# Two transformer blocks on one core: grouped attention products, early splits of the attention output, and the context's first modulation moved behind the last split of block 1

## The chip, the cores and the metric

The kernel runs on 1 core of one Trainium2 chip. The metric is the device time of one execution in microseconds (us). The engines are called by the profile's names: PE does the matrix products, DVE the elementwise work, ACT the functions of one input, POOL some elementwise work and DMA issues, SP issues most DMAs.

## The reference, cut to what matters

Two blocks run one after the other over 512 tokens of width 1024. Block 1 is one layer whose halves are an RWKV-7 recurrence (8 heads) and a stick-breaking attention (8 heads):

```python
h = rmsnorm(x, norm_g[l]) * (1.0 + scale[:, None, :]) + shift[:, None, :]
p = h @ w_in[l]
y = jnp.concatenate([y_rwkv, y_sb], axis=-1) @ w_out[l]
x = x + gate[:, None, :] * y
return rmsnorm(x, final_g)
```

Block 2 has two layers. Beside x it carries a context of 256 tokens, which has a modulation of its own. Layer 0 mixes with a short convolution, layer 1 with neighbourhood attention (16 heads, a window of keys and all of the context), and each ends in a gated feed-forward:

```python
h = _modulate(_rms_norm(x, norm_mix[i]), sh1, sc1)
hc = _modulate(_rms_norm(ctx, norm_mix[i]), sh1c, sc1c)
...
s = jnp.concatenate([s_win.reshape(bsz, N_HEADS, GRID_W, kh * GRID_W), s_ctx], axis=-1)
p = jax.nn.softmax(s, axis=-1).astype(v.dtype)
...
x = x + g1 * y
x = x + g2 * _swiglu(_modulate(_rms_norm(x, norm_ffn[i]), sh2, sc2), ffn_w_in[i], ffn_w_out[i])
```

Everything is fp32.

## The kernel before, in words

Activations lie transposed: eight tiles of 128 channels by 512 tokens for x, eight of 128 by 256 for the context (xc). A large product is made of three: each operand is split into a high part in the shorter format fp32r (a copy on ACT) and the low rest (a subtraction on DVE), and `mm3` (L172 to L174) adds high by high, high by low and low by high in one PSUM bank. `split_w` (L155, L156) does this for weights as they arrive by DMA in the SP queue; four slots hold 512-column pieces of split weights, so two weight tiles of 1024 columns are at hand at a time. `split` (L307, L308) does it for activations, and `modulate` (L288 to L291) for a normed and modulated tile: a product `nt` on DVE, a cast with the shift on ACT, a difference on DVE.

The kernel is written against a scheduler that lays out each engine's queue when the program is built. It takes ready instructions by the order of the program, with its own model of durations, so work that comes later in the text fills gaps of earlier work. `order(later, earlier)` adds an edge between two instructions that only this planning sees; no semaphore comes of it. Tiles with one tag share a fixed number of slots, and a tile waits for its slot. PSUM has eight banks, shared out by tag: in block 1 `acc` has two and six other tags have one each; in layer 1 `acc` 2, `cacc` 1, `sm` 2, `pt` 2, `py` 1.

The end of block 1 (`block1`, from L398). The output product takes the eight parts y in the order `YORD`, so y3 and y7 come last. The loop over `YORD` splits each part (h0 to h7 by name); when it comes to y3 it first issues the products of the six parts at hand for all eight output tiles (`part`), and loads `w2`, the weights of the last two parts. Ahead of that loop stands the context's norm and its `modulate` (tiles nt, hc0 to hc7), which layer 0 needs first. Behind the loop, for each of the eight output tiles, the products with y3 and y7 (h3, h7) follow, an addition into x (L452), a square on ACT (L455) and a weighted sum of squares (L458, L460) that a product with a matrix of ones closes into the bank `ss` (L462). Its inverse root (`rsqrt`: Ln, then Exp, both on ACT) is r, with which layer 0's h is modulated.

The last stick-breaking pair (`sb_pair(3)`) runs beside the last RWKV pair. Its Sigmoids (L1154, L1155) and the Ln and Exp of the RWKV pair's norm (L242, L249) need different function tables of ACT.

In `layer0` the sum of all squares (`self.scale`, L491) is added up on DVE beside the first products. These start with the context (`lead`, `ctx_first`).

Layer 1 (`layer1`) runs eight pairs of heads (`na_pair`). Each pair makes q and k, norms them, and then goes through four blocks of 128 queries: for each of its two heads the scores (L863, L864, bank `sm`), the bias and the row minimum on DVE (L868), Exp on ACT (L870), the scaling by the inverse sum on POOL (L872), four transposes on PE (L876, bank `pt`) and a copy out (L877). After every second block `na_values` multiplies with the values (L896, bank `py`). Output parts 0 to 6 are copied to `o0` to `o6` and split after the last pair, into slots of the attention's own tags; part 7 is split straight from PSUM. Then `attn_w_out` is multiplied, one output tile m after the other, with the last two in halves of 256 tokens, each followed by the addition into x (L769) and a square. The modulation for the feed-forward (`turn`) follows by halves.

The feed-forward (`ffn`, with `split=1` in layer 1) begins with `lead`, which makes gate and up product of hidden tile 0 in both `acc` banks. For tile i, `gemm2` makes the gate product, then Tanh on ACT (L643), a product on DVE (L644), the up product, and a product and split (L649, L307, L308).

Of the kernel before, what the change touches and what calls it, by code (L numbers as in the profile page):

```python
# [16 lines left out]
KT = 8  # L17
# [67 lines left out]
class K:  # L85
# [198 lines left out]
    def modulate(self, xs, ks, gain, mod, sh0, r, h, pool, tag, rstd, bufs=2):  # L284
        nc, n = self.nc, rstd.shape[1]
        for k in ks:
# [4 lines left out]
            nc.vector.scalar_tensor_tensor(h[k][1], t, sh, h[k][0].bitcast(F32),  # L291
                                           op0=ALU.add, op1=ALU.subtract)
# [17 lines left out]
    def block1(self):  # L310
# [68 lines left out]
        with self.open(name="sb", bufs=1) as sb:  # L379
# [22 lines left out]
            with self.open(name="tail", bufs=2) as tp:  # L402
# [9 lines left out]
                self.modulate(xc, range(KT), gc, mod, 0, 1, hc, tp, "cz", rstd)  # L412
                yh, part = [], []
                for k in YORD:
# [31 lines left out]
        for n, m in enumerate((6, 7, 0, 1, 2, 3, 4, 5)):  # L446
# [10 lines left out]
            if n == 0:  # L457
                nc.vector.tensor_scalar(acc, sq, fw[:, m:m + 1], None, op0=ALU.mult)  # L458
            elif n <= 5:
                nc.vector.scalar_tensor_tensor(acc, sq, fw[:, m:m + 1], acc, op0=ALU.mult, op1=ALU.add)  # L460
            if n >= 5:
                nc.tensor.matmul(ms, lhsT=self.C("ones") if n == 5 else fwt[:, n - 6], rhs=acc if n == 5 else sq,  # L462
                                 start=n == 5, stop=n == 7)
# [8 lines left out]
        self.modulate(xs, range(KT), g, mod, 0, 0, h, pool, "xz", r2)  # L472

    def layer0(self):
# [13 lines left out]
        for i in range(8):  # L488
            zs.append(self.conv_tile(i, st, pool, lead if i == 0 else None))
            if i < 7:  # L490
                nc.vector.tensor_add(self.scale, self.sqs[0] if i == 0 else self.scale, self.sqs[i + 1])  # L491
# [65 lines left out]
    def gemm2(self, src, h, hc, k0=0, k1=KT):  # L557
        po = self.psum("acc")
# [71 lines left out]
    def ffn(self, l, st, pool, parts, fin=None, split=0):  # L630
# [51 lines left out]
    def xgemm(self, src, h, k0=0, k1=KT):  # L682
        out = self.psum("acc")
# [22 lines left out]
    def layer1(self):  # L706
# [5 lines left out]
        with ExitStack() as es:  # L712
# [34 lines left out]
            os = [pool.tile([128, S], F32, name=f"o{k}") for k in range(KT - 1)] + [None]  # L747
# [530 lines left out]
```

## Time and profile before

| what | value |
|---|---|
| median of 3 runs | 2077.85 us (2076.53 to 2081.96) |
| the profiled execution's own time | 2080.14 us |
| its span, first to last instruction | 2078.4 us |
| granted TensorE clock, mean | 0.994 |
| end of block 1 and turn to layer 0 | about 455 to 515 us of the span |
| attention of layer 1 | about 1425 to 1665 us |
| output product and turn to the last feed-forward | about 1665 to 1729 us |

The profile is of one execution. A row of its timeline gives the start in us from the span's start, the duration, the engine, the line, the operation, what it writes and reads, the shapes and the count, and in brackets how long the engine had been idle and whose end it waited for. A matrix product's duration includes its drain, which overlaps with the next one; the rate is read from start to start. PEclk is the share of the TensorE clock that was granted.

### The profile page before, as it was taken

To read this page: it belongs to the slowest core of one execution; us is meant where nothing else is said; L and a number is where in the kernel's file an instruction comes from. 1 tells how busy PE (TensorE), PEld (TensorE's weight loads), DVE (VectorE), ACT (ScalarE), POOL (GpSimd) and SP (SyncE) were. 2 spreads that over 40 slices of the span, in tenths; PEclk is the share of its full clock that TensorE was granted. 3 is DMA by queue.
4 is the path that set the end of the run, shared out by engine and by line. 5 is a ranking of instruction groups with operands and counts; after the bars stand their busy time and mean duration, and the time that the engine had idled before them with its cause. 6 is when DMAs were issued, how large, how long until landed. Compare 5 with 4: busy or idle time off the path is not lost.

```text
span 2078.4 us, 33492 instructions
## 1 busy us (share of the span) xinstructions
PE 2029.1 (98%) x13564; PEld 1637.2 (79%) x13564; DVE 1230.9 (59%) x2641; ACT 795.6 (38%) x1493; POOL 131.5 (6%) x212
## 2 busy tenths in 40 slices
PE   6999999998999999999999999999999999999999
PEld 3766667666888888888888888898777687888887
DVE  2869888658766738675446343444666754444443
ACT  3536444446322224221222222335776743323232
POOL 0000000000000000000001000001223200000000
PEclk9999999999999999999999999999999999999999
DMA  7432222122233312344235221122111122323323
GB/s 280 150 113 92 94 74 93 40 81 83 92 122 122 122 61 93 131 133 151 94 135 177 72 96 61 58 82 67 56 52 51 36 82 82 101 93 97 98 98 103
DMA packets 61355, 203.59 MB, mean 98 GB/s; under 512 B 6928, under 2 KB 8976, under 8 KB 61200
## 3 DMA queue, kind: packets, MB, share of 16 engines
q1 hardware_dynamic: 45360, 145.77, 21.6%
q0 software_dynamic: 15120, 55.06, 8.1%
q8 instruction: 106, 1.74, 0.4%
q10 hardware_dynamic: 720, 0.62, 0.1%
q14 instruction: 49, 0.40, 0.1%
HBM read 199.32 MB, written 2.10 MB: 97 GB/s over the span
## 4 chain that ended last, share of the span: by engine, by line
PE 87%; ACT 3%; DVE 3%; issue 1%; POOL 0%; DMA 0%; POOLq 0%; DVEq 0%; ACTq 0%
PE acc L173 20%; PE acc L174 20%; PE acc L172 19%; PE cacc L174 5%; PE cacc L173 5%; PE cacc L172 5%; PE py L896 2%; PE pT L876 1%; PE ss L1150 1%; PE so L1172 1%; PE sm L863 1%; PE sm L864 1%; PE G L980 1%; DVE nt L288 1%; PE ss L1165 1%
## 5 line engine op out<-in xcount | busy, mean ns | idle before, releaser
L155 ACT CAST wh<-st 128x512 fp32r<-128x512 f32 (+2 forms) x481 | 292.1, 609 | 722.0 <-PE acc L173 283.2
L156 DVE TENSOR_TENSOR wl<-st,wh 128x512 fp32r<-128x512 f32 (+2 forms) x481 | 323.4, 674 | 350.7 <-ACT wh L155 347.4
L172 PE MATMUL acc<-xzzh,wh 128*128 128x512 f32 x352 | 138.8, 394 | 0.0
L174 PE MATMUL acc<-xzzh,wl 128*128 128x512 f32 x352 | 138.0, 392 | 0.0
L173 PE MATMUL acc<-xzzl,wh 128*128 128x512 f32 x352 | 138.0, 392 | 0.0
L210 DVE CUSTOM_DVE_ANT_0 junk<-ast,cb,vec 128x512 bf16<-128x512 f32 x168 | 125.0, 744 | 15.7 <-DMA ast<-in_w_ada_dram 13.6
L210 DVE CUSTOM_DVE_ANT_0 junk<-ast,cb,m 128x512 bf16<-128x512 f32 x168 | 125.5, 747 | 2.8
L200 POOL DMA_DIRECT2D ast<-in_w_ada_dram x96 | 50.7, 528 | 996.5 <-DVE m L210 887.1
L174 PEld LDWEIGHTS acc<-xzzh,wl 128*128 128x128 f32 x352 | 66.0, 188 | 14.8
L173 PEld LDWEIGHTS acc<-xzzl,wh 128*128 128x128 f32 x352 | 66.1, 188 | 13.5 <-issue 0.5
L172 PEld LDWEIGHTS acc<-xzzh,wh 128*128 128x128 f32 x352 | 66.1, 188 | 13.4 <-issue 0.5
L173 PE MATMUL acc<-h7l,wh 128*128 128x512 f32 (+1 forms) x164 | 65.2, 397 | 4.1 <-DVE h7l L308 4.1
L172 PE MATMUL acc<-h0h,wh 128*128 128x512 f32 (+1 forms) x164 | 65.6, 400 | 3.0 <-DVE fs L644 3.0
L173 PE MATMUL cacc<-czzl,wh 128*128 128x256 f32 x240 | 68.1, 284 | 0.0
L172 PE MATMUL cacc<-czzh,wh 128*128 128x256 f32 x240 | 67.7, 282 | 0.0
L174 PE MATMUL cacc<-czzh,wl 128*128 128x256 f32 x240 | 67.3, 280 | 0.0
L172 PE MATMUL acc<-h3h,wh 128*128 128x512 f32 (+1 forms) x164 | 65.1, 399 | 0.9 <-DVE x L452 0.9
L174 PE MATMUL acc<-h2h,wl 128*128 128x512 f32 (+1 forms) x164 | 65.8, 401 | 0.0
L174 PE MATMUL acc<-h0h,wl 128*128 128x512 f32 (+1 forms) x164 | 65.7, 401 | 0.0
L173 PE MATMUL acc<-h3l,wh 128*128 128x512 f32 (+1 forms) x164 | 65.4, 399 | 0.3 <-DVE h3l L291 0.3
L174 PE MATMUL acc<-h7h,wl 128*128 128x512 f32 (+1 forms) x164 | 65.1, 397 | 0.4 <-issue 0.4
L173 PE MATMUL acc<-h5l,wh 128*128 128x512 f32 (+1 forms) x164 | 65.4, 399 | 0.0
(731 smaller groups left out, 5539.4 us busy)
## 6 DMA issues: line engine op xcount, KB each, us to landing
ast<-in_w_ada_dram POOLq DMA_DIRECT2D x96, 512.0 KB, 3.8
st<-in_ffn_w_in_dram SPq DMA_DIRECT2D x88, 512.0 KB, 3.5
st<-in_ffn_w_out_dram SPq DMA_DIRECT2D x32, 448.0 KB, 3.4
st<-in_w_in_dram SPq DMA_DIRECT2D x24, 512.0 KB, 3.5
st<-in_conv_w_in_dram SPq DMA_DIRECT2D x24, 512.0 KB, 3.5
ast<-in_ada_n_dram SPq DMA_DIRECT2D x16, 512.0 KB, 8.9
st<-in_ffn_w_out_dram SPq DMA_DIRECT2D x16, 512.0 KB, 3.5
st<-in_w_qk_dram SPq DMA_DIRECT2D x16, 512.0 KB, 3.4
```

Of the source, the lines that this page charges most:

```text
L155: nc.scalar.copy(hi[:, :n], sl)
L156: nc.vector.tensor_tensor(lo[:, :n], sl, hi[:, :n].bitcast(F32), ALU.subtract)
L172: mm(out, lhsT=lh, rhs=rh, start=first, stop=False)
L173: mm(out, lhsT=lh, rhs=rl, start=False, stop=False)
L174: return mm(out, lhsT=ll, rhs=rh, start=False, stop=last)
L200: self.nc.gpsimd.dma_start(st, src)
L210: i = self.nc.vector.tensor_tensor_reduce(out=junk, in0=st[:, hs], in1=c[:, hs], scale=0.5, scalar=o if hf else self.V(bname, j), op0=ALU. ...
L288: nc.vector.scalar_tensor_tensor(t, xs[k], gain[:, k:k + 1], rstd, op0=ALU.mult, op1=ALU.mult)
L863: mm(o, lhsT=qh[:, e, qs], rhs=ks, start=True, stop=False)
L864: mm(o, lhsT=ql[:, e, qs], rhs=ks, start=False, stop=True)
L876: nc.tensor.transpose(pT[:, to], s[:, 128 * i:128 * i + 128], self.C("ident"))
L896: self.nc.tensor.matmul(po[r, cs], lhsT=v[:, r], rhs=pts[e][:, blk:blk + n].rearrange("p a t -> p (a t)"), start=i == 0, stop=i == len(wor ...
```

## The change

In words:

- `block1`: the context's `modulate` moves from ahead of the loop over `YORD` to behind it.
- `block1`, sum of squares: of eight squares, number 0, 2 and 4 are weighted and added on DVE as before; numbers 1, 3 and 5 are weighted on ACT into a tile `sw` and added by a product with the ones matrix; 6 and 7 as before. There are six such products in place of three.
- `sb_pair`: the first Sigmoid of the last step (pair 3, block 3, head 0) is ordered behind the Exp of the last RWKV pair's norm.
- `layer0`: the first addition of the plain sum of squares is ordered behind the last step of x's modulation.
- `na_pair`: scores and softmax of both heads come first, then the transposes of both, the first head's ordered behind the scaling of the second; the first head's value products are ordered behind the second head's copy.
- `layer1`: output parts 0 to 3 are split straight from PSUM at the end of their pair, into tiles of their own; 4 to 6 are copied as before and split in the last pair; 7 as before.
- The output product's tile m = 2 and the gate product of the last feed-forward's tile 1 are put in the bank `cacc`.
- The table set with Exp and Tanh is loaded right behind the last Exp of layer 1's second norm half.

```diff
@@ block1
-                self.modulate(xc, range(KT), gc, mod, 0, 1, hc, tp, "cz", rstd)
                 yh, part = [], []
                 for k in YORD:
...
                         part.append(t)
+                self.modulate(xc, range(KT), gc, mod, 0, 1, hc, tp, "cz", rstd)
...
-            elif n <= 5:
+            elif n in (2, 4):
                 nc.vector.scalar_tensor_tensor(acc, sq, fw[:, m:m + 1], acc, op0=ALU.mult, op1=ALU.add)
-            if n >= 5:
-                nc.tensor.matmul(ms, lhsT=self.C("ones") if n == 5 else fwt[:, n - 6], rhs=acc if n == 5 else sq,
-                                 start=n == 5, stop=n == 7)
+            elif n <= 5:
+                sw = pool.tile([128, S], F32, tag="xz", name="sw")
+                nc.scalar.activation(sw, sq, AF.Identity, scale=fw[:, m:m + 1])
+            if n not in (0, 2):
+                nc.tensor.matmul(ms, lhsT=fwt[:, n - 6] if n >= 6 else self.C("ones"),
+                                 rhs=sq if n >= 6 else acc if n == 4 else sw, start=n == 1, stop=n == 7)
@@ layer0
-                nc.vector.tensor_add(self.scale, self.sqs[0] if i == 0 else self.scale, self.sqs[i + 1])
+                add = nc.vector.tensor_add(self.scale, self.sqs[0] if i == 0 else self.scale, self.sqs[i + 1])
+                if i == 0:
+                    self.order(add, self.hlast)
@@ ffn
-                pg = lead[0] if lead else self.gemm2(w1[i], *hs)
+                pg = lead[0] if lead else self.gemm2(w1[i], *hs, tag="cacc" if split and i == 1 else "acc")
@@ layer1
-            os = [pool.tile([128, S], F32, name=f"o{k}") for k in range(KT - 1)] + [None]
+            oh = [self.hl(pool, S, f"o{k}") for k in range(4)]
+            os = [pool.tile([128, S], F32, name=f"o{k}") for k in range(4, KT - 1)]
...
             for p in range(8):
-                last = self.na_pair(p, W, h, hc, gq, va, vc, mask, bts, os[p], wp)
-            oh = []
-            for k, tag in enumerate(("qh", "kk", "pt0", "pt1") * 2):
-                t = wp.tile([128, 2, S], F32R, tag=tag, name="oh", bufs=2)
-                oh.append((t[:, 0], t[:, 1]))
-                if k < KT - 1:
-                    self.split(oh[k], os[k])
-            for a, b in ((slice(0, 448), slice(64, S)), (slice(448, S), slice(0, 64))):
-                self.split((oh[7][0][:, a], oh[7][1][:, a]), last[:, b])
+                po = self.na_pair(p, W, h, hc, gq, va, vc, mask, bts, wp)
+                if 4 <= p < KT - 1:
+                    nc.scalar.copy(os[p - 4][:, :448], po[:, 64:])
+                    nc.vector.tensor_copy(os[p - 4][:, 448:], po[:, :64])
+                    continue
+                if p == KT - 1:
+                    for k, tag in enumerate(("qh", "kk", "pt0", "qh")):
+                        t = wp.tile([128, 2, S], F32R, tag=tag, name="oh", bufs=2)
+                        oh.append((t[:, 0], t[:, 1]))
+                        if k < 3:
+                            self.split(oh[4 + k], os[k])
+                for a, b in ((slice(0, 448), slice(64, S)), (slice(448, S), slice(0, 64))):
+                    self.split((oh[p][0][:, a], oh[p][1][:, a]), po[:, b])
...
-                add(m, self.xgemm(A["attn_w_out"][m], oh), slice(0, S))
+                add(m, self.xgemm(A["attn_w_out"][m], oh, tag="cacc" if m == 2 else "acc"), slice(0, S))
...
-            self.rsqrt(rstd[:, hv[1]], sx["ps"][:, hv[1]])
+            done = self.rsqrt(rstd[:, hv[1]], sx["ps"][:, hv[1]])
+            self.order(nc.scalar.preload_act_table_set("exp_and_others"), done)
@@ na_pair
+            probs = []
             for e in range(2):
...
-                nc.gpsimd.tensor_scalar(s, s, st[:, 2:3], 1.0, op0=ALU.mult, op1=ALU.mult)
+                ready = nc.gpsimd.tensor_scalar(s, s, st[:, 2:3], 1.0, op0=ALU.mult, op1=ALU.mult)
+                probs.append(s)
+            for e, s in enumerate(probs):
                 pT = self.psum("pt", (128, 4, 128), "pT")
                 for i in range(4):
                     to = 1 - i if j == 3 and i < 2 else i
-                    nc.tensor.transpose(pT[:, to], s[:, 128 * i:128 * i + 128], self.C("ident"))
-                (nc.scalar.copy if e else nc.vector.tensor_copy)(pts[e][:, j % 2::2], pT)
+                    t = nc.tensor.transpose(pT[:, to], s[:, 128 * i:128 * i + 128], self.C("ident"))
+                    if e == 0:
+                        self.order(t, ready)
+                copied = (nc.scalar.copy if e else nc.vector.tensor_copy)(pts[e][:, j % 2::2], pT)
...
@@ na_values
+                if e == 0:
+                    self.order(o, ready)
@@ rwkv_pair
-        self.rsqrt(rs, pv, last, eps=1)
+        self.pexp = self.rsqrt(rs, pv, last, eps=1)
@@ sb_pair
-                nc.scalar.activation(sg[:, :n], pz[:, :n], AF.Sigmoid)
+                first = nc.scalar.activation(sg[:, :n], pz[:, :n], AF.Sigmoid)
+                if p == 3 and i == 3 and e == 0:
+                    self.order(first, self.pexp)
```

The functions keep their other lines; `modulate` returns its last instruction, and `gemm2` and `xgemm` take the bank's tag.

More of the change, by code (lines that the diff above doesn't have):

```diff
@@ L290, in modulate @@
             nc.scalar.activation(h[k][0], t, AF.Identity, bias=sh)
-            nc.vector.scalar_tensor_tensor(h[k][1], t, sh, h[k][0].bitcast(F32),
-                                           op0=ALU.add, op1=ALU.subtract)
+            last = nc.vector.scalar_tensor_tensor(h[k][1], t, sh, h[k][0].bitcast(F32),
+                                                  op0=ALU.add, op1=ALU.subtract)
+        return last
     def bsum(self, ps, x, hi, lo):
@@ L458, in block1 @@
                 nc.vector.tensor_scalar(acc, sq, fw[:, m:m + 1], None, op0=ALU.mult)
+            elif n in (2, 4):
+                nc.vector.scalar_tensor_tensor(acc, sq, fw[:, m:m + 1], acc, op0=ALU.mult, op1=ALU.add)
             elif n <= 5:
-                nc.vector.scalar_tensor_tensor(acc, sq, fw[:, m:m + 1], acc, op0=ALU.mult, op1=ALU.add)
-            if n >= 5:
-                nc.tensor.matmul(ms, lhsT=self.C("ones") if n == 5 else fwt[:, n - 6], rhs=acc if n == 5 else sq,
-                                 start=n == 5, stop=n == 7)
+                sw = pool.tile([128, S], F32, tag="xz", name="sw")
[3 more added lines that the diff above has]
+                                 rhs=sq if n >= 6 else acc if n == 4 else sw, start=n == 1, stop=n == 7)
             if n in (3, 7):
@@ L471, in block1 @@
         nc.vector.tensor_mul(g, g, self.V("final_g", 0, 8))
-        self.modulate(xs, range(KT), g, mod, 0, 0, h, pool, "xz", r2)
+        self.hlast = self.modulate(xs, range(KT), g, mod, 0, 0, h, pool, "xz", r2)
     def layer0(self):
@@ L555, in layer0, with gemm2 @@
                 nc.sync.dma_start(A["dbg_c0"][k], self.xc[k])
-    def gemm2(self, src, h, hc, k0=0, k1=KT):
-        po = self.psum("acc")
+    def gemm2(self, src, h, hc, k0=0, k1=KT, tag="acc"):
+        po = self.psum(tag)
         w = self.load_w(src[:, k0 * 128:k1 * 128], (k1 - k0) * 128)
@@ L680, in pgemm, with xgemm @@
         return self.xgemm(W[t], h)
-    def xgemm(self, src, h, k0=0, k1=KT):
-        out = self.psum("acc")
+    def xgemm(self, src, h, k0=0, k1=KT, tag="acc"):
+        out = self.psum(tag)
         self.gemm(out, src, dict((k0 + i, t) for i, t in enumerate(h)), k0, k1)
@@ L798, in layer1, with na_pair @@
             nc.sync.dma_start(A["out"][k], xs[k])
-    def na_pair(self, p, W, h, hc, gq, va, vc, mask, bts, oh, wp):
+    def na_pair(self, p, W, h, hc, gq, va, vc, mask, bts, wp):
         nc = self.nc
@@ L875, in na_pair, with na_values @@
                     to = 1 - i if j == 3 and i < 2 else i
-                    nc.tensor.transpose(pT[:, to], s[:, 128 * i:128 * i + 128], self.C("ident"))
-                (nc.scalar.copy if e else nc.vector.tensor_copy)(pts[e][:, j % 2::2], pT)
+                    t = nc.tensor.transpose(pT[:, to], s[:, 128 * i:128 * i + 128], self.C("ident"))
+                    if e == 0:
+                        self.order(t, ready)
+                copied = (nc.scalar.copy if e else nc.vector.tensor_copy)(pts[e][:, j % 2::2], pT)
             if j % 2:
-                self.na_values(p, j // 2, po, pts, va, vc)
-        if oh is None:
-            return po
-        nc.scalar.copy(oh[:, :448], po[:, 64:])
-        nc.vector.tensor_copy(oh[:, 448:], po[:, :64])
-    def na_values(self, p, half, po, pts, va, vc):
+                self.na_values(p, j // 2, po, pts, va, vc, copied)
+        return po
+    def na_values(self, p, half, po, pts, va, vc, ready):
         c0 = 256 * half
@@ L895, in na_values @@
                 cs = slice(c0 + 128 * col, c0 + 128 * (col + n))
-                self.nc.tensor.matmul(po[r, cs], lhsT=v[:, r],
-                                      rhs=pts[e][:, blk:blk + n].rearrange("p a t -> p (a t)"),
-                                      start=i == 0, stop=i == len(work) - 1)
+                o = self.nc.tensor.matmul(po[r, cs], lhsT=v[:, r],
+                                          rhs=pts[e][:, blk:blk + n].rearrange("p a t -> p (a t)"),
+                                          start=i == 0, stop=i == len(work) - 1)
+                if e == 0:
+                    self.order(o, ready)
     def mix(self, ps, mu, omu, out):
```

## The prediction

> **What bounds the kernel now.** I read the page first, then the waits of PE, then the windows around each wait, then the timeline inside them. PE is busy for nearly the whole span, so only what PE loses can be won.
>
> ```profile
> PE 2029.1 (98%) x13564; PEld 1637.2 (79%) x13564; DVE 1230.9 (59%) x2641; ACT 795.6 (38%) x1493; POOL 131.5 (6%) x212
> ```
>
> ```profile
> PE sm L260 <- DVE acc L259: 14.3, 1, 14.3
> PE acc L173 <- DVE h7l L308: 4.1, 1, 4.1
> PE acc L172 <- DVE fs L644: 3.0, 1, 3.0
> ```
>
> The columns are total, times and longest, in us. The first wait is the start of the program, which the change leaves alone. The other two stand where the change works: one product of block 1's output waits for the low half of the last output part (h7l), and the second feed-forward tile of layer 1 waits for DVE to empty a PSUM bank. The windows show what each costs beyond the wait.
>
> ```profile
> 491.00:511.50 20.50, 15.08 (x49) 10.18 (x47) 19.24 (x41) 10.64 (x21) 0.00 (x0) 0.83 0.17 52
> 497.00:503.24 6.24, 6.07 (x13) 4.29 (x14) 5.43 (x14) 2.83 (x6) 0.00 (x0) 0.50 0.09 35
> 1641.00:1651.00 10.00, 6.84 (x26) 4.79 (x26) 7.25 (x15) 6.48 (x13) 0.00 (x0) 0.83 0.17 53
> 1709.00:1721.50 12.50, 12.41 (x96) 11.70 (x94) 12.13 (x29) 7.99 (x19) 0.00 (x0) 1.00 0.27 84
> 1721.50:1728.80 7.30, 4.34 (x14) 3.33 (x13) 3.27 (x5) 3.32 (x5) 0.00 (x0) 0.77 0.44 144
> ```
>
> After the length come busy time of PE, weight loads, DVE, ACT and POOL, and then the granted clock. From 497 to 503.24 PE is "busy" at half clock: the throttle that the 4.1 us wait set off costs up to (1-0.50) x 6.24 = 3.1 us more and counts as work. But in the whole tail, 491 to 511.5, DVE is busy 19.24 of 20.50 us: there DVE is the bound, and PE's wait can't all be won. A product of 512 columns at full clock takes 0.23 us from start to start:
>
> ```profile
> 1571.05 0.39 PE L172 MATMUL acc<-h3h,wh 128*128 128x512 f32 x1
> 1571.28 0.40 PE L173 MATMUL acc<-h3l,wh 128*128 128x512 f32 x1
> ```
>
> **The change part by part.**
>
> **A, the tail of block 1.** Three edits meet here. First, the order edge puts the first Sigmoid of the last stick-breaking step behind the Exp of the last RWKV norm. ACT's timeline has the sets loaded in turn:
>
> ```profile
> 466.75 0.69 ACT L242 ACTIVATE Z<-rsm,epsb 128x512 f32<-128x512 f32 x1 [0.51 <-PE rsm L1096]
> 467.45 1.28 ACT L1154 ACT_TABLE_LOAD   x1
> 468.75 0.60 ACT L1154 ACTIVATE sg<-ss 128x512 f32<-128x512 f32 x1
> 469.36 1.28 ACT L249 ACT_TABLE_LOAD   x1
> 470.66 0.63 ACT L249 ACTIVATE Z<-Z 128x512 f32<-128x512 f32 x1
> 471.31 1.28 ACT L1155 ACT_TABLE_LOAD   x1
> 472.60 0.60 ACT L1155 ACTIVATE om<-ss 128x512 f32<-128x512 f32 x1
> ```
>
> Two of the three loads go. Ln ends at 467.44; then Exp 0.63, one load 1.28, sg 0.60, om 0.60 end at 470.55 instead of 473.20: 2.65 us earlier. What follows om to the last part y7 is one chain through one PSUM bank, so I let y7 and its split come 2.65 us earlier. The Trainium skill (ScalarE: Activation LUTs, What ACT_TABLE_LOAD costs) gives about 2.66 us for each switch, the load and a drain as long again. The rows have no drain: the load starts 0.01 us after Ln and sg 0.02 us after the load. With the page's figure two loads would be worth 5.3 us instead of 2.65, and the preload of part C below 2.66 instead of 1.28: a sum of about 15.6 instead of 14.3, by estimate.
>
> Second, the context modulation (eight products nt and eight differences on DVE, eight casts on ACT, no DMA) is issued behind the last split instead of ahead of it. It leaves DVE's work in the stretch as it was. What is late next is the eight additions x (L452), each of which frees a PSUM bank and is queued on DVE behind the modulation; PE waits for them instead of for h7l. So this edit alone brings no more than DVE's idle 20.50 - 19.24 = 1.26 us. Casts move with it on ACT, which is busy 10.64 of 20.50.
>
> Third, three of the five weighted additions L460 leave DVE.
>
> ```profile
> L452 DVE SCALAR_TENSOR_TENSOR x<-acc,m,part x6: 744/744/751, 502.2 to 510.7; 128x512 f32<-128x512 f32 x6
> L460 DVE SCALAR_TENSOR_TENSOR acc<-sq,fw,acc x5: 740/741/745, 504.9 to 510.1; 128x512 f32<-128x512 f32 x5
> ```
>
> ```profile
> 510.75 0.74 DVE L452 SCALAR_TENSOR_TENSOR x<-acc,m,part 128x512 f32<-128x512 f32 x1
> ...
> 511.00 1.15 ACT L455 ACTIVATE sq<-x 128x512 f32<-128x512 f32 x2
> ...
> 513.76 0.69 ACT L242 ACTIVATE r<-ss,epsb 128x512 f32<-128x512 f32 x1 [1.61 <-PE ss L462]
> ```
>
> That is 3 x 0.74 = 2.2 us off DVE. They become three ACT scalings (0.63 each by a square of that size, 1.9 of ACT's idle 9.9) and three more products with the ones matrix. Before, three such products ran from the last L460's end (510.84) to 513.76, 0.97 us each; so PE gets 2.9 us more, in a stretch where it waits for DVE. If that cover is gone it costs 2.9. The end gets shorter too: the last square ends at 512.15, one product later is 513.1, against 513.76: 0.65 us. Sum: 2.65 + 2.2 + 0.65 = 5.5; I take off 0.7 because DVE won't be gapless between PE's eight tiles: **4.8**. Ends: 2.2, if only DVE's lost work counts, since PE has block-1 products to do until 491.9 whenever y7 comes; 6.0, where PE binds (48 products at 0.23 and six at 0.97 make 16.9 of the 22.8 us from 491 to 513.76).
>
> The edge that holds layer 0's sum of squares behind the last modulation: three of its seven additions ran while DVE waited for r.
>
> ```profile
> 513.35 1.42 DVE L491 TENSOR_TENSOR r<-r,sq 128x512 f32<-128x512 f32 x2
> ```
>
> They come after instead. Others of them no longer stand between the modulation's steps, and PE is on the context's products meanwhile, so I take 0; without that cover it is 3 x 0.7 = 2.1.
>
> **B, the last attention pair.** Output parts 0 to 3 are split as they are made, into tiles of their own. Before, no split ran ahead of the last pair:
>
> ```profile
> L307 ACT CAST oh<-o x7: 602/619/623, 1639.5 to 1665.4; 128x512 fp32r<-128x512 f32 x7
> L308 DVE TENSOR_TENSOR oh<-o,oh x7: 672/689/693, 1640.2 to 1666.0; 128x512 fp32r<-128x512 f32 x7
> L307 ACT CAST oh<-py x2: 213/370/527, 1665.9 to 1667.3; 128x448 fp32r<-128x448 f32 x1, 128x64 fp32r<-128x64 f32 x1
> L308 DVE TENSOR_TENSOR oh<-py,oh x2: 214/416/617, 1666.6 to 1667.8; 128x448 fp32r<-128x448 f32 x1, 128x64 fp32r<-128x64 f32 x1
> ```
>
> ```profile
> PE sm L863 <- DVE kk L840: 1.9, 1, 1.9
> PE pt L298 <- ACT hsh L296: 1.6, 4, 0.6
> PE pT L876 <- POOL s L872: 1.4, 3, 0.7
> ```
>
> With no later pair to draw on, PE is idle 3.16 us of the ten from 1641, and a clock of 0.83 takes 1.7 more: 4.9 to be had. With four parts split, output tiles 0 and 1 offer 2 x 12 products at 0.23 = 5.5 us of filler, and tile 2 gets a third bank (cacc). Some of it is missing later, while the last part is awaited: **4.0**. Ends 4.9, and 1.0 if the weights of tile 1 come late. Their loads keep their order in SP's queue; they can only start sooner. An early split puts 0.21 us more on ACT and about 0.62 on DVE; at 59% busy DVE hides it, and four of them cost 3.3 if not.
>
> **C, into the feed-forward of layer 1.** The gate product of tile 1 goes to the free bank cacc and needn't wait for DVE's fs: the 3.0 us wait and (1-0.77) x 7.30 = 1.7 us of clock go, 4.7 together. 24 products at 0.23 (5.5 us) then cover Tanh and what frees the next bank. Its weights are there in time, at 1721.13:
>
> ```profile
> 1720.45 0.68 DVE L156 TENSOR_TENSOR wl<-st,wh 128x512 fp32r<-128x512 f32 x1
> ```
>
> Against it stands the preloaded table set, 1.28 us on ACT behind the last Exp, ahead of this cast and all behind it:
>
> ```profile
> 1711.36 0.49 ACT L290 ACTIVATE h4h<-nt,m 128x256 fp32r<-128x256 f32 x1
> ```
>
> In that window DVE (12.13 of 12.50) waits for these casts and PE (12.41) follows closely. I charge 1.2: **3.5**; ends 4.7 (hidden), 2.0 (1.5 more waits behind it).
>
> **D, grouping.** Both heads' transposes stand together, and both heads' value products. Before, products of other kinds stand between them:
>
> ```profile
> 1565.11 0.60 PE L876 MATMUL pT<-con,s 128*128 128x128 f32 x4
> 1565.47 0.48 PE L864 MATMUL sm<-kk,ql 128*128 128x512 f32 x1
> 1565.88 0.65 PE L896 MATMUL py<-pt,vc 128*64 128x256 f32 x2
> ```
>
> The one between takes 0.41 us to the next start, not 0.23: 0.18 for a break. I estimate four breaks fewer in a pair, 0.14 to 0.18 each, 4.6 us over eight pairs. The price is a wait: the first head's transposes are ordered behind the second head's scaling on POOL, and behind them on PE stands everything else.
>
> ```profile
> L872 POOL TENSOR_SCALAR s<-s,st 128x512 f32<-128x512 f32 x64 | 45.6, 720 | 211.6 <-DVE st L871 200.5 <-PE sm L864 5.4 <-PE pT L876 4.2
> ```
>
> Fully exposed, 32 x 0.72 = 23 us. The nearest row says it is hidden (transposes waited 1.4 us for POOL in all), so I take **2.0** gained, between 4.6 gained and 23 lost.
>
> Sum: 4.8 + 4.0 + 3.5 + 2.0 = 14.3. The profiled execution took 2080.14 (span 2078.4 and 1.7 around it): 2065.8. It was 2.3 above the median of the runs, 2077.85, so I forecast **2063.5**.
>
> **The rivals.**
> 1. DVE keeps the tail and grouping brings nothing: A 2.2, D 0. Sum 9.7: 2068.1. For it speaks 19.24 of 20.50; against, that y7 does come earlier.
> 2. The clock stays low in the tail. PE now waits there for each x instead of once. If that holds the clock at half as from 497 to 503, the last four tiles, 24 products, take 5.5 us more: A is -0.7, the sum 8.8, 2069.0. The Trainium skill (TensorE: Matmul & The Clock Gate, A second HAM failure mode: psum-queue depth-cycling) says that such micro-idles between groups do this. The 0.50 row came after one long wait; no row here shows it for short ones.
> 3. The waits re-form: x stands behind the modulation as h7l did (A 0.7), weights come late (B 1.0, C 2.3), D 0. Sum 4.0: 2073.8, no change that can be told. The order edges add no speed of their own, which speaks for it; the free banks speak against it.
> 4. Slower: PE, in order, stands before each pair of transposes until POOL has scaled the second head. A, B and C bring 12.3; from 12.3 / 32 = 0.38 us a group the change loses, and at the full 0.72 it ends at 2077.85 - 12.3 + 23 = 2088.6. Against it: the 1.4 us.
> 5. Better: the upper ends, 6.0 + 4.9 + 4.7 + 4.6 = 20.2: 2057.6.
>
> **How the numbers follow.** Forecast 0.52, rival 1 0.15, rival 2 0.08, rival 3 0.10, rival 4 0.05, rival 5 0.10. The forecast and rivals 1, 2 and 5 lie over 0.3% (6.2 us, about what a measurement of this kernel can tell from none) below 2077.85, rival 4 as far above: faster 0.85, same 0.10, slower 0.05. The range 2056 to 2072 leaves out rivals 3 and 4 and a little at each end. The forecast's own is 2060 to 2067.
>
> **What would show it.** A: no wait of over 1.5 us for h7l, two table loads fewer, two L460, Ln of r near 509 instead of 513.76, and waits of PE for x in their place. B: a clock over 0.95 in the last pair and output products ahead of its scores. C: no wait for fs L644, and one of under 1.5 us for h4 to h7. D: transposes in eights, with waits for POOL under 3 us. The prediction is wrong if DVE's queue holds x behind the whole modulation, if transposes wait for POOL more than 0.38 us each time, or if the preload starves the last products of layer 1's norm.

## The result, and the profile after

The changed kernel takes **2058.38 us** (median of four runs, 2056.85 to 2059.89) against 2079.15 for the kernel before in the same comparison (2076.53 to 2081.96): a ratio of 0.990, 95% interval 0.9883 to 0.9917. That is 20.8 us less. The forecast was 2063.5 in a range of 2056 to 2072: the direction and the range held, the forecast's own narrower range (2060 to 2067) did not. The profiled execution took 2058.18 us, span 2056.4, 22.0 less than the span of before. The page, and the waits of PE that answer to the three quoted of before:

```profile
PE 2014.4 (98%) x13570; PEld 1632.6 (79%) x13570; DVE 1231.3 (60%) x2638; ACT 794.0 (39%) x1494; POOL 129.9 (6%) x212
```

```profile
PE sm L260 <- DVE acc L259: 13.9, 1, 13.9
PE pt L299 <- ACT hsh L297: 3.0, 8, 0.5
PE acc L172 <- DVE x L453: 1.7, 3, 0.7
PE ss L466 <- ACT sq L456: 1.5, 1, 1.5
...
PE acc L172 <- ACT h4h L290: 1.3, 1, 1.3
...
PE pT L891 <- POOL s L885: 0.7, 3, 0.2
```

The waits for h7l (4.1) and fs (3.0) are gone. In their place stand waits for x of at most 0.7 us each and the 1.3 us for h4h that the preloaded table set was charged with. The wait for hsh grew from 1.6 to 3.0.

To see where the 22.0 us come from, both traces are cut at marks that both have: the Ln of the last RWKV norm, the Ln of r, the first context product of attention pair 0 and of pair 7, the first ones product of layer 1's norm, the end. The marks of after, then those of before that the prediction did not show:

```profile
463.85 0.69 ACT L242 ACTIVATE Z<-rsm,epsb 128x512 f32<-128x512 f32 x1 [0.50 <-PE rsm L1112]
...
508.67 0.69 ACT L242 ACTIVATE r<-ss,epsb 128x512 f32<-128x512 f32 x1 [1.22 <-PE ss L466]
...
1425.73 0.28 PE L172 MATMUL cacc<-hc0h,wh 128*128 128x256 f32 x1
...
1625.39 0.28 PE L172 MATMUL cacc<-hc0h,wh 128*128 128x256 f32 x1
...
1678.87 0.38 PE L280 MATMUL sm<-acc,con 128*128 128x256 f32 x1
```

```profile
1430.85 0.28 PE L172 MATMUL cacc<-hc0h,wh 128*128 128x256 f32 x1
...
1637.89 0.28 PE L172 MATMUL cacc<-hc0h,wh 128*128 128x256 f32 x1
...
1697.11 0.38 PE L280 MATMUL sm<-acc,con 128*128 128x256 f32 x1
```

The differences of these times, in us, for the two kernels and for all that follow below:

```
                 to Ln Z   tail   layer 0  7 pairs  last pair,  FFN of   from Ln Z
                                                    output      layer 1  to the end
before            466.75  47.01   917.09   207.04     59.22     381.20    1611.56
after             463.85  44.82   917.06   199.66     53.48     377.46    1592.48
d_only            467.10  46.45   917.09   199.96     58.72     381.22    1603.44
no_edges          464.81  44.80   917.11   207.34     52.91     377.50    1599.66
b_only            464.37  47.01   917.11   205.15     52.84     382.17    1604.28
rev_sig           465.06  47.41   917.08   199.90     53.44     377.44    1595.27
rev_sums          466.65  44.42   917.10   199.76     53.44     377.50    1592.22
rev_move          466.13  45.35   917.09   199.66     53.45     377.44    1592.99
four_ones         466.55  44.01   917.13   199.64     53.43     377.48    1591.69
no_preload        469.71  44.82   918.61   199.70     53.41     376.13    1592.67
join              461.76  44.79   917.08   197.73     62.16     377.48    1599.24
best_join         466.00  44.01   917.13   196.20     62.16     376.10    1595.60
best_join7        463.87  44.04   917.15   196.91     61.71     376.13    1595.94
best              468.47  44.02   917.15   199.57     53.42     376.15    1590.31
```

Two things are to be read from it. First, a stage that an edit leaves alone mostly repeats within 0.1 to 0.3 us, so effects of under 1 us can be read here, which the medians of whole runs, with their spread of 3 to 11 us, can't show. Layer 0 takes 917.06 to 917.15 in all profiles but no_preload's, whose clock was low in its first 4 us:

```profile
514.53:518.57 4.04, 3.30 (x15) 3.30 (x16) 2.53 (x4) 2.70 (x4) 0.00 (x0) 0.58 0.30 114
```

The changed tail takes 44.79 to 44.82 in the four kernels that have it. Two things repeat less well: the tail of before, in which the granted clock averaged 0.93 (46.45 and 47.01 in d_only and before, with the same instructions in the same order), and the seven pairs in the kernels with join (196.20 to 197.73, also with the same order). Second, the first column moves between 461.76 and 469.71 although PE, DVE, ACT and POOL carry out the same instructions in the same order up to there in all of these kernels. So the 22.0 us are 2.9 ahead of the change and **19.1 behind it**: tail 2.2, the seven pairs 7.4, last pair with the output 5.7, feed-forward 3.7. Most of the 2.9 is one place:

```profile
100.00:108.00 8.00, 6.65 (x151) 5.86 (x150) 4.34 (x13) 2.96 (x3) 0.00 (x0) 0.57 0.17 61
```

```profile
100.00:108.00 8.00, 6.83 (x280) 5.97 (x281) 6.00 (x15) 2.96 (x3) 0.00 (x0) 1.00 0.38 116
```

These are the same 8 us of the windows of before and of after. After the length come the busy times of PE, weight loads, DVE, ACT and POOL, then the granted clock: 0.57 in the first, 1.00 in the second, on the same sequence of work. PE got 151 products done in the one and 280 in the other, most of them small ones of 32 by 32. Like instructions start 0.4 us apart just ahead of this place and 2.5 to 2.8 us apart just behind it.

### The profile page after: what moved, and what is told of

Read it like the earlier page. It is cut to its first block, busy times and chain, and to the rows that moved or that the text cites. A ratio compares the mean times of both kernels' runs of the same rounds, so it can differ in the third digit from the quotient of the medians.

```text
span 2056.4 us, 33481 instructions
## 1 busy us (share of the span) xinstructions
PE 2014.4 (98%) x13570; PEld 1632.6 (79%) x13570; DVE 1231.3 (60%) x2638; ACT 794.0 (39%) x1494; POOL 129.9 (6%) x212
## 4 chain that ended last, share of the span: by engine, by line
PE 87%; ACT 3%; DVE 2%; issue 1%; POOL 0%; ACTq 0%; DVEq 0%; POOLq 0%
PE acc L173 20%; PE acc L174 20%; PE acc L172 20%; PE cacc L174 5%; PE cacc L173 5%; PE cacc L172 5%; PE py L910 2%; PE pT L891 1%; PE ss L1166 1%; PE so L1190 1%; PE sm L876 1%; PE sm L877 1%; PE G L996 1%; PE ss L1183 1%; PE py L1098 1%
## 5 line engine op out<-in xcount | busy, mean ns | idle before, releaser
L172 PE MATMUL acc<-h4h,wh 128*128 128x512 f32 (+1 forms) x163 | 64.3, 396 | 1.3 <-ACT h4h L290 1.3
L173 PE MATMUL acc<-h4l,wh 128*128 128x512 f32 (+1 forms) x163 | 65.1, 400 | 0.0
L174 PE MATMUL acc<-h3h,wl 128*128 128x512 f32 (+1 forms) x163 | 64.9, 398 | 0.0
```

What stands on the lines that cost most here:

```text
L172: mm(out, lhsT=lh, rhs=rh, start=first, stop=False)
L173: mm(out, lhsT=lh, rhs=rl, start=False, stop=False)
L174: return mm(out, lhsT=ll, rhs=rh, start=False, stop=last)
```

## The experiments

**What the grouping is worth alone (d_only, b_only), and what does it (no_edges).** d_only is the kernel before with this, and the same for the value products:

```diff
+            probs = []
             for e in range(2):
...
+                ready = nc.gpsimd.tensor_scalar(s, s, st[:, 2:3], 1.0, op0=ALU.mult, op1=ALU.mult)
+                probs.append(s)
+            for e, s in enumerate(probs):
...
+                    if e == 0:
+                        self.order(t, ready)
```

> The kernel before with the grouping of D alone (both heads' transposes together, both heads' value products together, with their order edges). The order that PE gets has 46 stretches of fp32 products (transposes, value products) among the fp32r products of the eight attention pairs, against 72 before and 47 in the changed kernel. Theory 1 (each stretch costs its entry and exit on PE): by the changed kernel's trace the first seven periods of a pair are 7.4 us shorter in all with 22 fewer stretches, some 0.34 us for each, so 26 fewer bring 8 to 9 us: about 2070. Theory 2 (the grouping is worth what the prediction gave it, 2.0 us at 0.14 to 0.18 a break, and the rest of the shorter pairs comes from the early splits, which spread DVE's work): 2 to 4.6 us, about 2075. Under both the wait of transposes for POOL stays under 2 us in all.

Measured: 2072.32 us (2067.17 to 2077.76), ratio 0.9965 (0.9952 to 0.9979). The seven pairs take 199.96 instead of 207.04, as in the changed kernel (199.66): 7.1 us there and 0.5 in the last pair. That is nearer theory 1 (8 to 9) than theory 2 (2 to 4.6); the grouping needs no other part.

b_only is the kernel before with the early splits of parts 0 to 3, those of parts 4 to 6 in the last pair, and output tile 2 in cacc.

> The kernel before with part B alone: early splits of output parts 0 to 3, the split of part 7 straight from PSUM, output tile 2 in the bank cacc. No grouping. Its PE order has 64 fp32 stretches in the attention against 72 before. Theory 1 (B is a matter of the last pair, the grouping of its own): from the start of the last pair's context product to the end of the output tiles 59.2 us become 53.5 to 54.5 (4.7 to 5.7 gained), and the seven periods before lose 1 to 2.5 us of their 207.0 for the few stretches fewer. Theory 2 (the early splits spread DVE's work and this is what shortened the pairs): the seven periods fall to 200 to 202. The prediction's number for B is 4.0.

Measured: 2069.91 us (2067.71 to 2074.80), ratio 0.9953 (0.9940 to 0.9965). Last pair and output take 52.84 instead of 59.22, the seven pairs 205.15 instead of 207.04, so theory 1, with a little more in the last pair than its 53.5; 1.0 us of it is lost again in the feed-forward (382.17 against 381.20). Its only wait left from the last pair on is the one for fs, and the low clock behind that wait lasts longer than in before: (1-0.62) x 9.00 = 3.4 us lost, against the 1.7 that the prediction read there.

```profile
PE acc L172 <- DVE fs L644: 3.0, 1, 3.0
```

```profile
1711.00:1720.00 9.00, 6.04 (x16) 4.82 (x16) 3.54 (x6) 3.82 (x6) 0.00 (x0) 0.62 0.33 117
```

no_edges is the changed kernel without its two order edges, `self.order(t, ready)` of the transposes and `self.order(o, ready)` of the value products.

> The changed kernel with both heads' transposes still written together, but without the two order edges (transposes behind the second head's scaling, value products behind the second head's copy). PE's order then has 76 fp32 stretches in the attention instead of 47. Theory 1 (the number of stretches is what counts, 0.34 us each): 29 more cost 8 to 10 us, about 2067 to 2068, the periods of a pair are back at 29.5 us. Theory 2 (writing them together is enough, the edges add only waits for POOL): no slower than the changed kernel, 2057 to 2059.

Measured: 2068.43 us (2066.29 to 2073.41), ratio 0.9951 (0.9937 to 0.9965). The seven pairs are back at 207.34, 7.7 us more than in the changed kernel: theory 1, a little under its 8 to 10. Writing the transposes together does nothing by itself: the planner pulls them apart again. The grouping's whole gain in these pairs is the edges'; it is the first one's, since a program without the second alone has the same instructions in the same order on every engine. And it isn't waiting that costs it. The waits of PE from pair 0 to the end of the output, first of no_edges, then of d_only:

```profile
PE pT L891 <- POOL s L885: 0.5, 2, 0.3
PE pt L299 <- ACT hsh L297: 0.3, 1, 0.3
```

```profile
PE pt L298 <- ACT hsh L296: 4.4, 8, 1.8
PE sm L864 <- DVE kk L840: 1.5, 1, 1.5
PE pT L879 <- POOL s L873: 1.2, 4, 0.5
PE acc L172 <- ACT wh L155: 0.4, 1, 0.4
PE acc L172 <- ACT oh L307: 0.2, 1, 0.2
```

The kernel with fewer waits (0.8 against 7.7 us) is slower in the seven pairs. I added up, from pair 0 to the first ones product of the norm, the times from each product's start to the next one's start, by what follows: the fp32 steps are those that begin with a transpose or a value product; the others are set against 0.2285, 0.1185 and 0.061 us for 512, 256 and 128 columns at full clock, 174.09 us in every kernel, and what they take beyond it is put down to what comes next.

```
              stretches  fp32     beyond full rate, ahead of            sum with
              of fp32    steps    transposes   values      fp32r        174.09
before           72      65.79    6.89 (49)    3.07 (23)   16.42        266.26
no_edges         76      65.08    6.46 (53)    2.94 (23)   11.69        260.26
b_only           64      63.89    4.59 (43)    2.79 (21)   12.62        257.99
after            47      62.61    2.39 (30)    1.76 (17)   12.28        253.13
d_only           46      62.94    2.56 (30)    1.55 (16)   17.53        258.68
join             20      65.68    1.79 (19)    0.10 (1)    18.23        259.89
```

Between before and after the column ahead of fp32r products, where most of the waits lie, falls by 4.1, and the three fp32 columns fall by 9.0. That is a split by kind of product, and not one by edit. d_only lowers the fp32 columns by 8.7 and raises the other by 1.1; b_only, which groups nothing, lowers the fp32 columns too, by 4.5, with eight stretches fewer, and the other by 3.8. The two edits overlap: alone they bring 7.6 and 8.3 us in this part of the trace, together 13.1.

In the seven pairs before has 64 stretches of fp32 products and after 41; 7.4 us for 23 fewer are 0.32 us a stretch, or 0.16 for each of its two changes of kind. The 6 fewer of b_only come to 0.31 each, the 29 more of no_edges against after to 0.27. The count isn't everything, though: no_edges has six stretches more than before and takes only 0.3 us longer there. No run changes the number of changes of kind and nothing else, so it is argued from these counts, and not shown, that they are the cause.

**Does it go on like that? (join).** Value products of a half pair right behind a group of transposes, so that two stretches become one (the copies and splits of a part follow its values):

```diff
-            if j % 2:
-                self.na_values(p, j // 2, po, pts, va, vc, copied)
-        return po
+            if j == 0 and p and True:
+                self.pend(t)
+            if j == 1:
+                first = pts
+            if j == 2:
+                self.na_values(p, 0, po, first, va, vc, t)
+        return po, lambda t: self.na_values(p, 1, po, pts, va, vc, t or copied)
```

> The changed kernel with the value products of a half pair put right behind a group of transposes: those of the first half behind the transposes of the third query block, those of the second half behind the first group of transposes of the next pair. PE's order then has 20 fp32 stretches in the attention instead of 47. Theory 1 (a stretch costs PE 0.27 to 0.32 us, as the seven periods of before, after, no_edges and b_only have it): 23 or so fewer in the seven periods make 199.7 us to 192.3 to 193.5, and 27 fewer in all bring 7 to 9 us: about 2050. Theory 2 (the gain of the grouping came from fewer waits and a fuller queue, not from the stretches): the seven periods stay at 198 to 200 us and new waits for pt appear.

Measured: 2063.46 us (2062.17 to 2066.96), ratio 0.9927 (0.9910 to 0.9943): some 5 us behind the changed kernel. Theory 1 falls as a rule of its own. Theory 2's new waits for pt came, but the seven pairs got a little shorter than it said (197.73). But 58 products fewer lie between their marks, and the last pair takes 62.16 instead of 53.48. Over both, 259.89 against 253.14. The last row of the table above shows why: the entries into fp32 did go (1.89 us left of 4.15), but the fp32 steps are 3.1 us longer and what stands ahead of fp32r products 5.9 us. PE now waits inside the attention, where the changed kernel had 3.0 us for hsh and 0.7 for s:

```profile
PE pT L896 <- POOL s L890: 3.6, 9, 0.5
PE pt L299 <- ACT hsh L297: 3.4, 8, 1.1
PE pt L299 <- DVE pt L899: 1.0, 2, 0.6
PE pt L299 <- ACT pt L899: 0.4, 1, 0.4
```

That makes 4.7 of the 6.8 us lost; the rest is not told apart. The 1.4 us for pt are not fixed: the same order without them comes below (best_join). This is the price that the prediction feared of the grouping itself (waits for POOL), and it came at the next step of it.

**The tail of block 1, edit by edit (rev_sig, rev_sums, rev_move).** Each is the changed kernel with one of the three edits taken back.

```diff
-                if p == 3 and i == 3 and e == 0:
-                    self.order(first, self.pexp)
```

> The changed kernel without the order edge that puts the first Sigmoid of the last stick-breaking step behind the Exp of the last RWKV norm, so that two more table loads of 1.28 us come back. Theory 1 (y7 is a chain and its delay is passed on in full): Ln of r comes 2.6 us later than in the changed kernel. Theory 2 (PE has products of block 1 to do until the end of the window and the tail is bound by PE or DVE): under 0.8 us later.

Measured: 2064.77 us (2062.19 to 2066.18), ratio 0.9928 (0.9916 to 0.9941). The tail takes 47.41 instead of 44.82: 2.59 us, two loads at 1.30. The delay is passed on in full, theory 1.

```diff
-            elif n in (2, 4):
+            elif n <= 5:
                 nc.vector.scalar_tensor_tensor(acc, sq, fw[:, m:m + 1], acc, op0=ALU.mult, op1=ALU.add)
-            elif n <= 5:
-                sw = pool.tile([128, S], F32, tag="xz", name="sw")
-                nc.scalar.activation(sw, sq, AF.Identity, scale=fw[:, m:m + 1])
-            if n not in (0, 2):
...
+            if n >= 5:
...
```

> The changed kernel with the old weighted sum of squares in the tail of block 1: five additions on DVE and three products with the ones matrix, instead of two additions and six products. Theory 1 (DVE is the bound of the tail, as the prediction had it): three additions of 0.74 and the longer end come back, Ln of r is 2.2 to 2.9 us later than in the changed kernel when counted from the first table load of the tail. Theory 2 (in the changed kernel PE is the bound at the end: three ones products of 0.93 us stand between and ahead of the last tile's six products, and DVE waits 3.18 us for PE before the last x): what DVE loses PE wins, Ln of r is between 0.5 us earlier and 0.8 us later.

Measured: 2060.32 us (2057.21 to 2064.40), ratio 0.9908 (0.9892 to 0.9923). The tail takes 44.42, 0.4 us **less** than with the new sums. Theory 2. (It is one trace, but the four with the new sums lie within 0.03 us.) What the edit took off DVE it put on PE, at the end, where PE had become the bound. The changed kernel's last two tiles, PE and then DVE:

```profile
501.88 1.02 PE L466 MATMUL ss<-acc,con 128*128 128x512 f32 x2
502.74 1.02 PE L466 MATMUL ss<-sw,con 128*128 128x512 f32 x2
503.20 0.80 PE L172 MATMUL acc<-h3h,wh 128*128 128x512 f32 x1
503.83 1.02 PE L466 MATMUL ss<-sq,fwt 128*128 128x512 f32 x2
504.29 0.79 PE L173 MATMUL acc<-h3l,wh 128*128 128x512 f32 x1
...
505.62 0.39 PE L174 MATMUL acc<-h7h,wl 128*128 128x512 f32 x1
507.51 1.12 PE L466 MATMUL ss<-sq,fwt 128*128 128x512 f32 x2 [1.50 <-ACT sq L456]
```

```profile
506.05 0.75 DVE L453 SCALAR_TENSOR_TENSOR x<-acc,m,part 128x512 f32<-128x512 f32 x1 [3.18 <-PE acc L174]
```

Three ones products stand ahead of or between the last tile's six products, and DVE is idle for 3.18 us until the last sum is there. With the old sums it is the other way round, PE waits for DVE's last addition:

```profile
PE ss L463 <- DVE acc L461: 2.8, 1, 2.8
```

rev_move has the line `self.modulate(xc, ...)` back ahead of the loop over the splits.

> The changed kernel with the context modulation back ahead of the splits. Theory 1 (DVE does the same work in either order): the tail, 44.8 us from the last Ln of the RWKV norm to Ln of r, changes by under 0.5 us; PE waits for h7l again and less for x. Theory 2 (the prediction's bound for this edit alone, 1.26 us, is used): 0.8 to 1.3 us longer.

Measured: 2059.86 us (2056.77 to 2064.35), ratio 0.9902 (0.9887 to 0.9917). The tail takes 45.35, 0.5 us more; PE waits for x 2.5 us in two waits instead of 1.7 in three, and not for h7l, against what theory 1 said of that wait. Its size lies between the theories, within the bound of 1.26. DVE's queue says why the wait stays away. The making of y7 and the low half of its split, in before and then in rev_move:

```profile
490.06 1.11 DVE L1183 TENSOR_TENSOR y<-ors,sgs 128x512 f32<-128x512 f32 x1
...
496.24 0.69 DVE L308 TENSOR_TENSOR h7l<-y,h7h 128x512 fp32r<-128x512 f32 x1
```

```profile
487.08 1.08 DVE L1201 TENSOR_TENSOR y<-ors,sgs 128x512 f32<-128x512 f32 x1
488.07 0.88 DVE L288 SCALAR_TENSOR_TENSOR nt<-xc,gc,rstd 128x256 f32<-128x256 f32 x2
488.86 0.69 DVE L309 TENSOR_TENSOR h7l<-y,h7h 128x512 fp32r<-128x512 f32 x1
```

In before twelve instructions stand between the two, 6.18 us from start to start; in rev_move it is two, 1.78 us, as in the changed kernel. The planner lets the split come early although the modulation is written ahead of it. In rev_sig too it follows after 2.24 us. So none of the three edits taken back brings the 4.1 us wait back, nor the half clock behind it (1.00 in the tail of all three); no run puts in one of them alone, and which of them removed the wait stays open. Taken singly the three edits are worth 2.6, -0.4 and 0.5 us; together, by before and after, 2.2.

**Two edits that this points to (four_ones, no_preload), and all of it (best_join, best_join7, best).** four_ones keeps four weighted additions on DVE, scales square number 5 on ACT and puts all ones products behind `tail`, the last tile's last product:

```diff
+            elif n <= 4:
+                nc.vector.scalar_tensor_tensor(acc, sq, fw[:, m:m + 1], acc, op0=ALU.mult, op1=ALU.add)
+            elif n == 5:
+                sw = pool.tile([128, S], F32, tag="xz", name="sw")
+                nc.scalar.activation(sw, sq, AF.Identity, scale=fw[:, m:m + 1])
...
+            if n == 7:
+                for a, b, f, l in ((self.C("ones"), acc, True, False), (self.C("ones"), sw, False, False),
+                                   (fwt[:, 0], sqs[6], False, False), (fwt[:, 1], sq, False, True)):
+                    self.order(ones(a, b, f, l), tail)
```

> The changed kernel with four products with the ones matrix in the tail of block 1 instead of six, all behind the last tile's products: the weighted sum of four squares stays on DVE (four additions instead of two), the fifth square is scaled on ACT. Theory 1 (PE's two products of 0.93 fewer, and none of them ahead of the last tile): the tail, 44.8 us from the last Ln of the RWKV norm to Ln of r, is 1.0 to 2.5 us shorter. Theory 2 (DVE, with two additions of 0.66 more, is as late as PE was): within 0.5 us of 44.8, as with five additions (44.4).

Measured: 2060.07 us (2057.85 to 2065.38), ratio 0.9905 (0.9890 to 0.9919). Tail 44.01: 0.8 us less, between the theories. PE still waits 1.6 us for DVE's last addition.

no_preload is the changed kernel without this line:

```diff
-            self.order(nc.scalar.preload_act_table_set("exp_and_others"), done)
```

> The changed kernel without the preloaded table set in the norm of layer 1. The wait of 1.3 us of PE for the cast h4h should go, and the table load stands ahead of the first Tanh of the feed-forward instead. Theory 1 (the 24 products of tile 1's gate cover that load): the stretch from the attention's output to the end, 377.5 in the changed kernel, is 1.0 to 1.4 us shorter. Theory 2 (the load is then exposed there, or the wait re-forms at the next cast): 377.2 to 378.8.

Measured: 2059.70 us (2055.41 to 2064.21), ratio 0.9897 (0.9881 to 0.9913). The feed-forward's stage takes 376.13, 1.33 us less: theory 1. No wait of PE is left in it ahead of tile 1, and the load stands here:

```profile
1710.51 0.62 ACT L155 CAST wh<-st 128x512 fp32r<-128x512 f32 x1 [1.38 <-PE acc L173]
1711.14 1.28 ACT L649 ACT_TABLE_LOAD   x1
1712.44 0.60 ACT L649 ACTIVATE fs<-acc 128x512 f32<-128x512 f32 x1
```

So the bank cacc for tile 1 and the preload answer the same wait, and with the bank the preload only costs.

> The kernel join with two things more: four ones products in the tail of block 1, behind the last tile (0.8 us in four_ones), and no preloaded table set (1.3 us in no_preload). By addition of the stages 2.1 us less than join: about 2048 if theory 1 holds there, 2056 if theory 2 holds.

> The kernel best_join without the order edge of the transposes in the last pair. In no_edges the stretch from the last pair's context product to the end of the output tiles was 0.57 us shorter than in the changed kernel. If the edge holds fillers back there (theory 1), 0.3 to 0.6 us less than best_join in that stretch; if a stretch more costs as elsewhere (theory 2; 22 instead of 20), 0.5 us more.

Measured: 2062.89 (2059.45 to 2066.26) and 2062.52 us (2061.30 to 2065.22), ratios 0.9922 (0.9905 to 0.9939) and 0.9923 (0.9905 to 0.9940). The 0.8 and 1.3 us are there again (44.01, 376.10), and join's loss stays. It is smaller here: the seven pairs take 196.20 and 196.91 instead of 197.73, although all three kernels have the same order of instructions in them. The waits for pt come and go with it, 1.4 us in join, none in best_join and 0.7 in best_join7. All waits of PE in the attention of best_join:

```profile
PE pT L898 <- POOL s L892: 3.6, 9, 0.5
PE pt L299 <- ACT hsh L297: 3.5, 8, 1.1
```

Without the last edge the last pair is 0.45 us shorter, but the seven pairs are 0.7 us longer although the edit concerns the last one alone, so that this pair of runs doesn't decide.

> The changed kernel with three things that the other runs pointed to: four ones products in the tail of block 1 (0.8 us less in four_ones), no preloaded table set (1.3 us less in no_preload), and no order edges in the last pair (0.57 us less there in no_edges). Theory 1 (the stages add up): tail 44.0, seven periods 199.7, last pair to the end of the output tiles 52.9, from there to the end 376.1, together 2.7 us less than the changed kernel over the same stages, about 2056. Theory 2 (the last pair's gain in no_edges came from its other neighbours): 53.4 there, 2.1 us less in all.

Measured: 2058.50 us (2057.06 to 2060.60), ratio 0.9896 (0.9879 to 0.9912). From Ln Z to the end 1590.31, 2.17 less than the changed kernel: theory 2, the last pair stays at 53.42. Over the whole program the medians show no difference from the changed kernel's 2058.38, taken in another comparison: the profiled run of this one was at Ln Z 4.6 us later. By its stages it is the best of the kernels; that it is faster as a whole is not shown.

## Why the prediction was right, and where it was not

The sum, 14.3 us, came out at 19.1 behind the change. That the total lay in the range was partly luck: A brought 2.6 us less than its term, B 1.2 and D 5.6 more, and such misses need not offset each other.

- **Before's own time.** The 2.3 us taken off, because the profiled run was slower than the median, fit the trace: that run lost about as much to the clock at 100 to 108 us, against the profile of after. Eight of the fourteen profiles have a low clock near there (0.83 to 0.91 from 100 to 120 us), so the close match is in part luck. And "Ln of r near 509", which came out as 508.67, looked right for a wrong reason: 2.9 of its 5.1 us lie ahead of the tail.
- **A, 4.8 forecast, 2.2 measured,** the lower end. Two table loads went and passed on 2.6 (2.65 forecast); no wait for h7l, two L461, waits for x in its place, all as said. The reason given, the move of the modulation, isn't shown: without it the wait stays away and the waits for x are there (2.5 us); the move alone is worth 0.5, within its bound. The step that failed is the third: three additions off DVE (2.2) and the shorter end (0.65), with the three more ones products hidden "in a stretch where it waits for DVE". Measured -0.4. The sentence "If that cover is gone it costs 2.9" was the right one: with three ones products the end of the tail waits for DVE, with six DVE waits for PE, and both end within 0.4 us. The Trainium skill (ScalarE: Activation LUTs, What ACT_TABLE_LOAD costs) would have made two loads worth 5.3; the 2.59 of rev_sig and the 1.33 of no_preload are the load's 1.28 each and no drain.
- **The order edge into layer 0, 0 forecast:** the stage takes 917.06 against 917.09.
- **B, 4.0 forecast, 5.2 measured** as the difference of after and d_only in the last pair and the output, a little over the upper end of 4.9 (6.4 alone, in b_only). The prediction left out that the early splits shorten the other pairs too: b_only's take 1.9 us less, with six stretches of fp32 products fewer. The clock in the last pair is full, as forecast:

```profile
1629.00:1640.00 11.00, 10.64 (x53) 8.72 (x54) 9.11 (x16) 8.66 (x18) 0.00 (x0) 1.00 0.14 48
```

- **C, 3.5 forecast, 3.7 measured.** The bank is worth 5.1 (381.20 to 376.13 with no_preload), the preload costs 1.33 (1.2 charged). What the prediction did not see is that the bank covers the load too.
- **D, 2.0 forecast, 7.6 measured** alone (d_only); taking the edges back costs 7.7 in the seven pairs. The price was about right: 0.13 to 0.16 us a change of kind, against 0.14 to 0.18. The count failed: "four breaks fewer in a pair" are 6.6 (23 stretches of two changes each over seven pairs). And I then took less than half of it, for waits for POOL that didn't come: 0.7 us in all, less than the 1.4 of before. The transposes stand mostly in eights, as forecast (38 groups for 256); no_edges shows that the order edges, which I took for the risk, are what brings the gain.
- **The rivals.** Rival 1 had A right (2.2) and D wrong (0). Rival 2, a clock low in the tail, did not come: 1.00 from 485 to 508.7, with three waits for x of up to 0.7 us. The Trainium skill (TensorE: Matmul & The Clock Gate, A second HAM failure mode: psum-queue depth-cycling) tells of micro-idles between groups of products that make the clock swing between half and full; these three waits did nothing of the kind. Rival 3's waits for x came (1.7 us), its sum did not; rival 4's for POOL not here, but in join. Rival 5's time, 2057.6, was the nearest, though A lay at the lower end and D far over its upper one.

```profile
485.00:508.70 23.70, 20.37 (x72) 12.58 (x70) 19.19 (x43) 13.95 (x27) 0.00 (x0) 1.00 0.21 70
```

## What to carry to other kernels

Before work is moved from the busy engine to the idle one, ask who is the bound once all the other edits are in: here an edit was forecast at 2.9 us from the profile of before, and was worth -0.4 in the kernel that it went into. Count changes of kind in the order that an engine really gets, from the trace or the program, not from the source: writing two groups together changed nothing until an order edge held them together, and one step more of it lost more to new waits than it won. Where whole runs differ by several us, cut the trace at marks that both kernels have; stages that no edit touches tell how far such a difference can be trusted. And look where the planner put an instruction: with the modulation written back ahead of it, the split of y7 stayed where it was in DVE's queue.

## What was not expected of the hardware

- The granted clock averaged 0.57 over 8 us in one execution and 1.00 in another at the same place of the same work. Up to the last RWKV norm the profiles differ by up to 8 us (461.76 to 469.71), while 917 us of dense products repeat within 0.1 in 13 of 14.
- A wait of PE of 2.8 us (rev_sums, for acc) left the clock at 1.00; the wait of 3.0 us for fs was followed by 0.77 over 7.3 us in before and by 0.62 over 9.0 us in b_only.
- Ahead of a transpose PE loses 0.14 us beyond the full rate in before (49 times, 6.89 us) and 0.08 in after (30 times, 2.39), waits for POOL of 1.4 and 0.7 us included: the price of a change of kind is not one constant.
